# A hybrid layer on one core: in the recurrence, the two chunks of a block trade places for odd pairs of heads

## The chip, the cores and the metric

One core of a Trainium2 chip runs the whole layer. The metric is the device time of one execution in microseconds (us); before, it is 2475.47 us, the median of three runs. A profile of one execution stands beside it.

## What is computed

One decoder layer on 2048 tokens of 1024 channels: a mixer of two groups of heads (an SSD group and an RWKV-7 group), then a convolved GLU. The change lies in the RWKV-7 group. Cut to what matters here, its 8 heads of 64 channels each run this recurrence over the tokens:

```
def step(S, inp):                       # S: 64 x 64 for each head
    r_t, w_t, k_t, v_t, a_t, b_t = inp
    sa = jnp.einsum("bhij,bhj->bhi", S, a_t)
    S = S * w_t[:, :, None, :] + sa[..., None] * b_t[:, :, None, :] + v_t[..., None] * k_t[:, :, None, :]
    return S, jnp.einsum("bhij,bhj->bhi", S, r_t)
...
y = _rwkv7_scan(rh, heads(decay), kh, vh, -kk, kk * ah)
y = ((y - mean) * lax.rsqrt(var + RWKV_GN_EPS)).reshape(b, T, RWKV_D) * f32(ln_w) + f32(ln_b)
```

The vectors r, k, v, w, a and the gate come from projections of the normalised input (`xn @ w_in`) and small products behind them.

## The kernel before

The 2048 tokens are 16 **blocks** of 128; a block is two **chunks** of 64 tokens. The 8 heads are 4 **pairs** j, and hh (0 or 1) is the head within a pair. Tensors with channels on the 128 partitions (`tk`, `tr`, `tv`, `AR`, `BK`) hold a pair's two heads in the two halves of the partitions and the block's 128 tokens along the row, chunk 0 first.

Within a chunk the recurrence is solved in matrix form. `gram` makes the masked products `G` of a chunk (128 partitions: one half for the solved vectors U, one for the values V). `sides(c)` says which: for chunk 0 the U half is partitions 64 to 127 (`us`) and the V half 0 to 63 (`vs`), for chunk 1 the other way round. `UV[:, c]` holds U and V of a chunk in the same halves. Per chunk these steps follow each other; their products are small and in fp32, and the trace shows each fp32 product as two records:

- `own`: `local` (L1306) multiplies the V half of `G` by V, for the `us` and the `vs` columns of every head (16 products of 64 x 64 on a 64-column operand), into the bank `pq`; `past` (L1312) adds the state's part, 4 full products; then ScalarE copies the `us` half of `pq` to `qs` (L1318).
- `update`: 8 products with the inverse `XT` (L1330), all in the same 64 x 64 quarter of the array, into `pu`; ScalarE copies them to the U half of `UV` (L1334, one instruction of 64 x 512).
- `state`: `kept` on GpSimd scales the old state, `fresh` (L1354, `pS`, 8 products of 128 rows by 64 columns, left and right half of the array in turn), `join` on VectorE adds both (L1360); `reads` (L1365) multiplies the U half of `G` by U into the `vs` half of `pq`, 8 products in one and the same quarter; ScalarE copies that half to `ysb` (L1371).

`XT` comes from a chain of 62 small VectorE instructions for each block (`solve`, L1186 and L1192, `tmp` and `xl`), with DMAs before and behind; `turn` (L1257, `XW`, on VectorE) and `merge` (L1273 `pw`, L1277 `po`, tiles of 32 x 32 at opposite corners of the array: rows from 64 to columns from 96 and rows from 0 to columns from 32, and their mirror images) finish the inverse. `values` makes the centred V (L1239, `vt`, 4 full products) and the bonus (L1247, `bo`, one product on 512 columns). The big products are the projections `d` (to `tk`, `tr`, `tv` and others) and `c` (for the convolution), L735, 24 at a time.

TensorE's order is written out by hand. For blocks 1 to 13 a list (`PLAN`) interleaves, in one **period**, the steps of block f (`f.`), of the one behind it (`b.`) and of the one behind that (`a.`); the other engines issue in the order of the same list. So every engine runs its queue in order, and an instruction that waits holds back what stands behind it on its engine. In a period TensorE runs, in this order: `nq` (a norm), `local` of chunk 0, `c`, `past`, `c`, `pw`, `c`, `po`, `gr` (the gram), `pu`, `c`, `zg`, `pS`, `reads`, `c`, `local` of chunk 1, `past`, `bt`, `d`, `pu`, `bt`, `d`, `reads`, `pS`, `d`, `bo`, `d`, `yt`, `vt` and `d` to the next `nq`. Lists of their own (`HEAD`, `ORDER`) do the same for the start and the end. Behind the recurrence come the SSD chunks and the GLU.

Of the kernel before, what the change touches and what calls it, by code (L numbers as in the profile page):

```python
# [10 lines left out]
AF = mybir.ActivationFunctionType  # L11
# [7 lines left out]
P = 128  # L19
# [256 lines left out]
R0.merge.1/0 R1.gram.1/0 R1.conv.5/0 R0.merge.1/1 R0.update.0/0 R1.conv.5/1 R1.gram.1/1 R1.gram.1/2 R1.conv.3/8  # L276
R1.receptance/2 R2.load/0 R1.conv.3/9 R1.conv.6/0 R1.conv.3/10 R1.conv.1/11 R2.load/3 R1.receptance/4 R1.conv.5/2
R1.solve/0 R1.conv.5/4 R0.update.0/1 R1.conv.5/3 R1.conv.5/5 R1.receptance/3 R1.solve/1 R1.conv.5/7 R1.solve/3
R1.solve/2 R2.load/4 R1.conv.7/0 R1.conv.3/11 R1.solve/8 R2.load/5 R2.load/6 R0.state.0/2 R0.merge.1/2
R1.transposed.0/0 R1.conv.7/1 R1.conv.5/6 R1.conv.5/8 R0.state.0/5 R0.own.1/0 R1.d.10/0 R1.solve/4 R0.state.0/3  # L280
R1.conv.7/2 R1.conv.7/4 R0.state.0/4 R1.conv.7/6 R1.receptance/1 R0.state.0/6 R1.conv.7/3 R1.solve/7 R0.own.1/1
R2.load/7 R0.gate/0 R1.solve/5 R0.own.1/2 R0.update.1/0 R0.update.1/1 R0.state.1/5 R0.state.1/6 R0.finish.0/0
R0.state.1/0 R0.state.1/1 R1.solve/6 R1.d.11/0 R1.conv.7/8 R1.conv.7/5 R1.conv.7/7 R1.d.11/1 R1.solve/9 R1.solve/10
R1.solve/11 R1.conv.5/9 R1.solve/12 R1.solve/13 R1.solve/14 R1.solve/15 R1.solve/16 R1.solve/17 R1.solve/18
R1.solve/19 R1.solve/20 R1.solve/21 R1.solve/22 R1.solve/23 R1.solve/24 R1.solve/25 R1.solve/26 R1.solve/27
R1.solve/28 R1.solve/29 R1.solve/30 R1.solve/31 R1.conv.7/9 R0.state.1/2 R1.solve/32 R1.solve/33 R1.solve/34
# [33 lines left out]
f.d.11/1 f.solve/7 n.load/8 b.update.1/0 b.update.1/1 f.solve/9 f.d.11/2 f.solve/10 f.solve/11 f.solve/12 f.solve/13  # L320
f.solve/14 f.solve/15 f.solve/16 f.solve/17 f.solve/18 f.solve/19 f.solve/20 f.solve/21 f.solve/22 f.d.11/3 f.solve/23
f.solve/24 f.solve/25 f.solve/26 f.solve/27 f.solve/28 f.solve/29 f.solve/30 f.solve/31 f.solve/32 f.solve/33
f.solve/34 n.load/9 f.transposed.1/0 f.d.12 f.d.11/4 b.state.1/5 b.state.1/2 f.d.13/0
# [416 lines left out]
def phase_R(tc, K, const, tables, x, w_r, w_c, wl_d, g2_d, XN, XC, YR, iters=16):  # L740
    nc = tc.nc
    V, S, G_ = nc.vector, nc.scalar, nc.gpsimd
    with ExitStack() as ctx:
# [102 lines left out]
        def bank(name, tag, bufs=1):  # L846
# [1971 lines left out]
```

## Time and profile before

| | before |
|---|---|
| runs | 2476.57, 2471.09, 2475.47 us; median 2475.47 us |
| the profiled execution | 2477.94 us, its span 2476.2 us |
| TensorE busy | 2386.1 us, 96% of the span |
| VectorE, ScalarE, GpSimd busy | 1876.3, 1193.2, 1061.6 us |
| blocks 1 to 13 in their periods | from 149.3 to 802.4 us, about 50.3 us each |
| the recurrence with start and end | to about 900 us; then SSD chunks to about 1240 us, GLU to the end |

Engines are named PE (TensorE), PEld (its weight loads), DVE (VectorE), ACT (ScalarE), POOL (GpSimd). A row of a timeline gives a group's start, its time from first start to last end, engine, line, operation, output and inputs, shapes and the number of records; idle time before it and what ended it stand in brackets. Matmuls overlap: the time from one row's start to the next row's start is what a group costs TensorE.

### The profile page before, as it was taken

The page shows a single profiled execution, that of the slowest core. Times are in us where ns is not written, and L with a number is a line of the kernel's source. Part 1 is how long each engine was busy: PE and PEld are TensorE (multiplying, and loading weights), DVE is VectorE, ACT ScalarE, POOL GpSimd, SP SyncE. Part 2 cuts the span into 40 slices and gives each one's busy share as a digit, 9 for nine tenths or more (in the row PEclk, how much of TensorE's full clock was granted, in tenths as well). Part 3 has the DMA queues.
Part 4 walks back from the last instruction along what each step waited for, and adds up shares of the span by engine and source line. Part 5 has one row for each costly group of instructions (what it writes and reads, how often), then busy time and mean ns, then how long its engine had stood idle before and what let it go on. Part 6 is the DMA issues. An engine that isn't in the chain of part 4 may idle for free.

```text
span 2476.2 us, 53715 instructions
## 1 busy us (share of the span) xinstructions
PE 2386.1 (96%) x21212; PEld 1513.2 (61%) x21212; DVE 1876.3 (76%) x3790; ACT 1193.2 (48%) x2407; POOL 1061.6 (43%) x1134
## 2 busy tenths in 40 slices
PE   4999999999999999999988999999989999999998
PEld 4899999999999755555533444444434444444443
DVE  6878777878787667678999799988988645546457
ACT  7556665666666444445555544444543432313132
POOL 3334443444434522223335658576755432313225
PEclk8999999999999999999999999999999999999999
DMA  7432333223422546565775444534455453333243
GB/s 226 91 68 57 79 72 77 58 63 78 87 58 62 172 122 169 154 175 164 194 225 172 166 151 152 182 136 153 149 175 174 166 162 98 107 102 102 85 158 111
DMA packets 344412, 319.12 MB, mean 129 GB/s; under 512 B 203232, under 2 KB 248672, under 8 KB 340832
## 3 DMA queue, kind: packets, MB, share of 16 engines
q1 hardware_dynamic: 344016, 315.43, 43.6%
q8 instruction: 166, 2.72, 0.5%
q14 instruction: 86, 0.70, 0.1%
q10 hardware_dynamic: 144, 0.26, 0.0%
HBM read 187.85 MB, written 110.99 MB: 121 GB/s over the span
## 4 chain that ended last, share of the span: by engine, by line
PE 40%; DVE 7%; issue 3%; POOL 2%; DMA 2%; ACT 2%; SPq 0%; DVEq 0%; POOLq 0%; ACTq 0%
PE u L2250 25%; PE d L2490 12%; DVE w L2103 1%; PE o L1964 1%; DVE C L2272 1%; PE l L2615 1%; DVE p L2307 1%; DVE a L2307 1%; POOL fa L2101 1%; DMA hs<-HN 0%; PE z L1749 0%; DVE dw L2454 0%; DMA HN<-hT 0%; POOL m L2002 0%; ACT hl L1983 0%
## 5 line engine op out<-in xcount | busy, mean ns | idle before, releaser
L2250 PE MATMUL u<-b,w 128*128 128x512 f16 x3696 | 807.0, 380 | 17.7 <-DVE C L2272 7.6
L2250 PEld LDWEIGHTS <-w 128*128 128x128 f16 x3696 | 362.3, 98 | 457.2 <-issue 24.4
L735 PE MATMUL d<-xt,wr 128*128 128x129 f16 x5376 | 334.6, 224 | 27.4 <-DMA xt<-xh 14.1
L735 PEld LDWEIGHTS <-wr 128*128 128x128 f16 x5376 | 319.9, 100 | 41.2 <-issue 33.1
L2490 PE MATMUL d<-dw,fa 128*128 128x512 f16 x1512 | 334.6, 380 | 4.3 <-DVE dw L2454 3.5
L2490 PEld LDWEIGHTS <-fa 128*128 128x128 f16 x1596 | 156.4, 98 | 199.6 <-issue 12.5
L2272 DVE TENSOR_TENSOR C<-u,C 128x512 f32<-128x512 f32 x220 | 150.8, 686 | 158.9 <-PE u L2250 141.9
L735 PE MATMUL c<-xt,wc 128*128 128x131 f16 x3072 | 194.3, 224 | 5.9 <-ACT tv L965 2.9
L735 PEld LDWEIGHTS <-wc 128*128 128x128 f16 x3072 | 182.1, 98 | 10.7 <-issue 6.1
L2503 DVE TENSOR_TENSOR acc<-d,acc 128x512 f32<-128x512 f32 x212 | 139.7, 683 | 43.8 <-PE d L2490 39.6
L2101 POOL TENSOR_TENSOR fa<-p,fa 128x512 f16<-128x512 f32 x100 | 133.6, 1346 | 74.4 <-ACT fa L2096 74.4
L2307 DVE SCALAR_TENSOR_TENSOR p<-C,fpar,p 128x1024 f32<-128x1024 f32 x88 | 121.2, 1377 | 45.4 <-ACT p L2303 45.2
L2103 DVE SCALAR_TENSOR_TENSOR w<-us,w 128x512 f16<-128x512 f32 x132 | 127.6, 977 | 9.3 <-ACT w L2096 8.6
L1014 DVE SCALAR_TENSOR_TENSOR ca<-c,cw,ca 128x128 f32<-128x128 f32 x360 | 114.5, 345 | 25.7 <-ACT ca L1004 21.8
L2268 ACT ACTIVATE C<-u 128x512 f32<-128x512 f32 x88 | 52.2, 594 | 169.5 <-PE u L2250 127.2
L2307 DVE SCALAR_TENSOR_TENSOR a<-C,fpar,a 128x1024 f32<-128x1024 f32 x88 | 121.8, 1384 | 6.9 <-ACT a L2303 5.5
L1186 DVE TENSOR_TENSOR tmp<-atl,xl 128x60 f32<-128x60 f32 (+24 forms) x465 | 117.0, 252 | 11.5
L1192 DVE TENSOR_TENSOR xl<-xl,tmp 128x60 f32<-128x60 f32 (+24 forms) x465 | 111.2, 239 | 13.9
L2096 ACT ACTIVATE fa<-p 128x512 f16<-128x512 f32 x110 | 65.6, 622 | 114.9 <-DVE p L2320 87.7
L2096 ACT ACTIVATE w<-us 128x512 f16<-128x512 f32 x132 | 79.9, 623 | 81.5 <-PE u L2250 31.4
L2223 POOL TENSOR_TENSOR us<-us,us 128x512 f32<-128x512 f32 x51 | 78.1, 1533 | 50.0 <-DVE w L2103 29.5
L1749 PE MATMUL z<-ws,xs 128*128 128x512 f16 x384 | 92.5, 383 | 0.0
(334 smaller groups left out, 4229.6 us busy)
## 6 DMA issues: line engine op xcount, KB each, us to landing
UW<-w SPq DMA_DIRECT2D x154, 256.0 KB
w<-UW SPq DMA_DIRECT2D x154, 256.0 KB
us<-in_w_u_dram SPq DMA_DIRECT2D x88, 256.0 KB
DW<-dw SPq DMA_DIRECT2D x70, 256.0 KB
dw<-DW SPq DMA_DIRECT2D x56, 256.0 KB
hs<-HN SPq DMA_DIRECT2D x48, 256.0 KB
r<-in_w_d_dram SPq DMA_DIRECT2D x10, 1024.0 KB
xin<-in_x_dram SPq DMA_DIRECT2D x16, 512.0 KB
```

The costliest lines, as they stand in the source:

```text
L735: nc.tensor.matmul(ps, w[:, a, kt, :], xt[:, b, kt, cols], start=n == 0, stop=n == 3 * KT - 1)
L1014: V.scalar_tensor_tensor(out=acc[:, q], in0=m["rc", e][:, q, k:k + 128], scalar=cw[:, e + q, k:k + 1], in1=acc[:, q], op0=ALU.mult, op1=AL ...
L1186: chain.tensor_tensor(out=self.tmp[:, :k, :n], in0=self.atl[:, j, j + 1:32].unsqueeze(1).to_broadcast([P, k, n]), in1=self.xl[:, :k, j:j + ...
L1192: chain.tensor_tensor(out=self.xl[:, :k, j + 1:32], in0=self.xl[:, :k, j + 1:32], in1=self.tmp[:, :k, :n], op=ALU.add)
L2096: S.activation(h, src, AF.Copy, **({} if scale is None else {"scale": scale}))
L2101: {"V": V, "G": G_}[engine].tensor_tensor(out=l, in0=src, in1=h, op=ALU.subtract)
L2103: V.scalar_tensor_tensor(out=l, in0=src, scalar=scale, in1=h, op0=ALU.mult, op1=ALU.subtract)
L2250: nc.tensor.matmul(bk[at], self.w[i][:, u, k, :], self.half.b[i][:, k, v, :], start=start and n == 0, stop=n == 11, skip_group_check=True)
L2272: op("V", .61, lambda: V.tensor_tensor(out=part(j, x), in0=bk[at], in1=part(*a), op=ALU.add), (("u", 4 * s + at), (*(c0, c1)[a[0]], a[1])) ...
L2307: V.scalar_tensor_tensor(out=o[j], in0=C[j][:, 2 - d:1026 - d], scalar=cw(g, 2 - d), in1=o[j], op0=ALU.mult, op1=ALU.add)
L2490: nc.tensor.matmul(bk[s, t], pairs[m].a[i][:, u, t * P:t * P + P], pairs[m].w[n][0][:, v, :], start=new and m == 0 and u == v == 0, stop=m ...
L2503: V.tensor_tensor(out=acc[j][:, t], in0=bk[s, t], in1=acc[j][:, t], op=ALU.add)
```

## The change

For odd pairs j the two chunks of a block are stored in swapped places: chunk 1's tokens first. A step for chunk c then works at place `c ^ j % 2`, so even pairs use one half of the partitions for U and odd pairs the other. With the heads taken in the order 0, 2, 1, 3, 4, 6, 5, 7, products that follow each other in `local` and `update` lie in opposite quarters of the array.

- `d`, `low` (tanh) and `finish` (affine) read the odd pairs with the two halves of 64 tokens swapped (a view with a reversed step of 64), or write them back so: the same instructions with another view.
- `local` makes the `us` columns alone, 8 products for 16. `reads` takes all 128 rows of `G` (U and V part at once), 8 products of 128 rows by 64 columns, left and right half of the array in turn.
- `qs` copies all 128 partitions (128 x 512). The copies to `UV` and to `ysb` become two each (`put(0)`, `put(1)`, 64 x 256).
- `vt` becomes 8 products with 64 columns of weights; `bo` becomes 6 products, of 128, 64 and 64 columns and the same again. `kept` on GpSimd has a view with one more dimension.
- In the lists the second copies stand behind the first; `R0.merge.1/2`, `R14.values/2`, `R15.values/2` and `R15.merge.1/2` move forward.

```
+        ORDER8 = (0, 2, 1, 3, 4, 6, 5, 7)
+        def swap(t):
+            return t.rearrange("p (c t) -> p c t", t=64)[:, ::-1]
...
                 def own(u):
-                    S.activation(dst(u), m["d", e][:, u, 1:129], AF.Identity, scale=omu[:, e + u:e + u + 1])
+                    S.activation(put(u), got(m["d", e][:, u, 1:129], u), AF.Identity, scale=omu[:, e + u:e + u + 1])
...
                     for j in range(4):
-                        nc.tensor.matmul(ps[:, j, :], self.tv[:, j], cmat, start=True, stop=True)
+                        for i in range(2):
+                            o = 64 * (i ^ j % 2)
+                            nc.tensor.matmul(
+                                ps[64 * i:64 * i + 64, j, :], self.tv[:, j, o:o + 64], cmat, start=True, stop=True)
...
-                    nc.tensor.matmul(m["bo"], K.bones, self.tr, start=True, stop=True)
+                    for j in range(4):
+                        for a, b in (((0, P),), ((0, 64), (64, P)))[j % 2]:
+                            o = 64 - a if j % 2 else a
+                            nc.tensor.matmul(
+                                m["bo"][:, j, a:b], K.bones, self.tr[:, j, o:o + b - a], start=True, stop=True)
...
+            def heads(self, c):
+                for n, h in enumerate(ORDER8):
+                    j, hh = h // 2, h % 2
+                    yield n, h, j, hh, c ^ j % 2, slice(h * 64, h * 64 + 64)
...
-                        for o in (us, vs):
-                            nc.tensor.matmul(
-                                pq[o, h * 64:(h + 1) * 64], self.G[vs, c, hh, j, o], self.UV[vs, c, h * 64:(h + 1) * 64],
-                                start=h == 0, stop=False, skip_group_check=True)
+                    for k, h, j, hh, i, q in self.heads(c):
+                        us, vs = self.sides(i)
+                        nc.tensor.matmul(
+                            pq[us, q], self.G[vs, i, hh, j, us], self.UV[vs, i, q], start=k < 2, stop=False,
+                            skip_group_check=True)
...
-                    S.activation(m["qs", c][us], m["pq", c][us], AF.Copy)
+                    S.activation(m["qs", c], m["pq", c], AF.Copy)
...
-                            pu[us, h * 64:(h + 1) * 64], self.XT[us, 4 * hh + j, :], m["qs", c][us, h * 64:(h + 1) * 64],
-                            start=True, stop=True)
-                return [products, lambda: S.activation(self.UV[us, c, :], m["pu", c][us], AF.Copy)]
+                            pu[us, q], self.XT[us, 4 * hh + j, :], m["qs", c][us, q], start=True, stop=True)
+                def put(b):
+                    us, vs = self.sides(c ^ b)
+                    S.activation(pick(self.UV[us, c ^ b, :], b), pick(m["pu", c][us], b), AF.Copy)
+                return [products, lambda: put(0), lambda: put(1)]
...
-                            m["pq", c][vs, h * 64:(h + 1) * 64], self.G[us, c, hh, j, vs],
-                            self.UV[us, c, h * 64:(h + 1) * 64], start=False, stop=h == 7, skip_group_check=True)
+                            m["pq", c][vs, q], self.G[:, i, hh, j, vs], self.UV[:, i, q], start=False, stop=k > 5,
+                            skip_group_check=True)
```

TensorE in the middle of a period, where `pS` and `reads` of chunk 0 stand between the gate `zg` and a group of `c`. Before:

```order
L735 MATMUL c_4_7938<-xt_6477,wc 128x131
L1380 MATMUL zg_8069<-GL_6402,g_200 128x128 x4
L1354 MATMUL pS_8078<-UV_7646,BT_7423 64x64 x8
L1365 MATMUL pq_7758<-UV_7646,G_7002 64x64 x8
L735 LDWEIGHTS wc
```

Now:

```order
L737 MATMUL c_4_7921<-xt_6471,wc 128x131
L1414 MATMUL zg_8053<-GL_6392,g_200 128x128 x4
L1386 MATMUL pS_8062<-UV_7637,BT_7405 64x64 x8
L1396 MATMUL pq_7749<-UV_7637,G_6989 64x64 x8
L737 LDWEIGHTS wc
```

Nothing moves there; `reads` (L1396, before L1365) keeps its number of products and has the shape of `pS` now. Then TensorE at chunk 1's `local` and `past`. Before:

```order
L735 MATMUL c_6_8110<-xt_6477,wc 128x131
L1306 MATMUL pq_8166<-UV_7646,G_7002 64x64 x16
L1312 MATMUL pq_8166<-S_1_228,AR_6953 128x128 x4
L1226 MATMUL bt_7_8194<-cst,BK_7886 128x128 x4
L735 LDWEIGHTS wr
```

Now:

```order
L737 MATMUL c_6_8094<-xt_6471,wc 128x131
L1334 MATMUL pq_8151<-UV_7637,G_6989 64x64 x8
L1340 MATMUL pq_8151<-S_1_228,AR_6939 128x128 x4
L1243 MATMUL bt_7_8171<-cst,BK_7869 128x128 x4
L737 LDWEIGHTS wr
```

The 16 products are 8 at the same place. Last, ScalarE between the copy to `UV` and the copy to `ysb` of chunk 0; `xh` and `xin` load the next block's input. Before:

```order
L1334 ACTIVATE UV_6616<-pu_6980 64x512
L916 ACTIVATE xh_6998,ss_6999<-xin_6956 128x1024
L1020 ACTIVATE ct_2_7045<-ca_2_6950 128x256
L1004 ACTIVATE ca_4_7066<-c_4_6908,cb,cw 128x128
L935 ACTIVATE xin_6956<-xin_6956,pnr_7013 128x1024
L936 ACTIVATE xh_6998<-xin_6956 128x1024
L1004 ACTIVATE ca_4_7066<-c_4_6908,cb,cw 128x128
L1382 ACTIVATE tg_7107<-zg_7039 128x512
L1371 ACTIVATE ysb_7134<-pq_6728 64x512
L1004 ACTIVATE ca_6_7161<-c_6_7080,cb,cw 128x128 x2
```

Now:

```order
L1362 ACTIVATE UV_6610<-pu_6966 64x2x128 x2
L926 ACTIVATE xh_6985,ss_6986<-xin_6942 128x1024
L1036 ACTIVATE ct_2_7032<-ca_2_6936 128x256
L1020 ACTIVATE ca_4_7053<-c_4_6894,cb,cw 128x128
L945 ACTIVATE xin_6942<-xin_6942,pnr_7000 128x1024
L946 ACTIVATE xh_6985<-xin_6942 128x1024
L1020 ACTIVATE ca_4_7053<-c_4_6894,cb,cw 128x128
L1416 ACTIVATE tg_7094<-zg_7026 128x512
L1402 ACTIVATE ysb_7121<-pq_6722 64x2x128 x2
L1020 ACTIVATE ca_6_7141<-c_6_7067,cb,cw 128x128 x2
```

Each copy is two, in the place of the one. VectorE, GpSimd and the DMA queue keep their order throughout, and TensorE and ScalarE theirs from the SSD chunks on.

## Rows read from the trace of the kernel before

**Rows 1.** The page's 40 slices of the span (62 us each): busy tenths of TensorE, and the granted clock of TensorE in tenths.

```profile
PE   4999999999999999999988999999989999999998
...
PEclk8999999999999999999999999999999999999999
```

**Rows 2.** Busy time by stretch: stretch, its length, then busy us (and instructions) of PE, PEld, DVE, ACT, POOL, then granted clock, DMA share and GB/s. The stretch before block 1, two periods, and the two stretches behind the periods.

```profile
110.00:149.40 39.40, 37.95 (x595) 35.18 (x596) 28.87 (x107) 21.51 (x51) 13.67 (x14) 1.00 0.33 66
149.40:199.70 50.30, 50.30 (x852) 47.38 (x854) 39.78 (x129) 31.17 (x71) 21.32 (x24) 1.00 0.30 64
...
400.70:451.00 50.30, 50.30 (x850) 47.36 (x849) 39.84 (x130) 31.16 (x71) 21.28 (x24) 1.00 0.32 71
...
803.10:853.40 50.30, 47.15 (x696) 39.91 (x694) 31.87 (x85) 25.64 (x52) 30.43 (x73) 1.00 0.57 183
853.40:900.00 46.60, 42.13 (x383) 26.25 (x382) 29.40 (x69) 24.77 (x62) 12.09 (x13) 0.92 0.48 147
```

**Rows 3.** TensorE's timeline in one period (the sixth), from `local` of chunk 0 to the product behind `vt`.

```profile
400.71 1.15 PE L1306 MATMUL pq<-UV,G 64*64 64x64 f32 x32
...
408.44 0.83 PE L1273 MATMUL pw<-XW,G 32*32 32x32 f32 x32
...
410.71 0.69 PE L1277 MATMUL po<-XT,XW 32*32 32x32 f32 x32
411.33 2.08 PE L1146 MATMUL gr<-AR,BK 64*128 64x128 f32 x32
413.35 1.14 PE L1330 MATMUL pu<-qs,XT 64*64 64x64 f32 x16
414.42 1.57 PE L735 MATMUL c<-xt,wc 128*128 128x131 f16 x24
...
416.87 0.69 PE L1354 MATMUL pS<-UV,BT 128*64 128x64 f32 x16
417.49 1.14 PE L1365 MATMUL pq<-UV,G 64*64 64x64 f32 x16
418.56 2.97 PE L735 MATMUL c<-xt,wc 128*128 128x131 f16 x48
421.46 1.15 PE L1306 MATMUL pq<-UV,G 64*64 64x64 f32 x32
422.54 1.16 PE L1312 MATMUL pq<-S,AR 128*128 128x128 f32 x8
...
431.56 4.31 PE L735 MATMUL d<-xt,wr 128*128 128x129 f16 x72
435.70 1.08 PE L1247 MATMUL bo<-tr,cst 128*128 128x512 f32 x2
436.68 1.54 PE L735 MATMUL d<-xt,wr 128*128 128x129 f16 x24
...
438.49 1.06 PE L1239 MATMUL vt<-cmat,tv 128*128 128x128 f32 x8
439.39 1.54 PE L735 MATMUL d<-xt,wr 128*128 128x129 f16 x24
```

**Rows 4.** TensorE's timeline in the SSD part: fp32 products with full weights on 64 columns.

```profile
878.73 1.90 PE L1881 MATMUL py<-Xdt,Dt 128*128 128x64 f32 x16
```

**Rows 5.** Operations with views in several pieces and plain ones beside them (groups by line with their shapes: busy us, mean ns of one).

```profile
L1123 POOL TENSOR_TENSOR BK<-tk,Pv 128x512 f32<-128x512 f32 x16 | 21.2, 1322 | 2.5 <-PE nq L1100 1.9 <-DVE tk L1116 0.6
L1428 POOL TENSOR_TENSOR yln<-yln,tv 128x512 f32<-128x512 f32 x16 | 20.8, 1302 | 69.4 <-ACT yln L1418 69.4
L1133 DVE TENSOR_TENSOR AR<-tr,Pi 128x512 f32<-128x512 f32 x16 | 10.8, 674 | 0.0
L1758 ACT ACTIVATE sz<-z 128x512 f32<-128x512 f32 x16 | 9.5, 593 | 12.4 <-PE z L1749 12.4
```

**Rows 6.** ScalarE's timeline in the same period, from the copies behind `pw` to the first instruction of the last group of `c`.

```profile
409.43 0.76 ACT L1284 ACTIVATE XW<-pw 32x256 f32<-32x256 f32 x2
...
414.53 0.59 ACT L1334 ACTIVATE UV<-pu 64x512 f32<-64x512 f32 x1 [2.32 <-PE pu L1330]
415.14 1.06 ACT L916 ACTIVATE xh<-xin 128x1024 bf16<-128x1024 f32 x1
...
420.48 0.58 ACT L1371 ACTIVATE ysb<-pq 64x512 f32<-64x512 f32 x1
421.57 0.81 ACT L1004 ACTIVATE ca<-c,cb,cw 128x128 f32<-128x128 f32 x2 [0.51 <-PE c L735]
```

**Rows 7.** VectorE's timeline in the same period: from the norm behind `nq` to `XW`, then from the first instruction behind the last `c` to the one that `nq` of the next period waits for by way of ScalarE.

```profile
404.87 0.69 DVE L1113 SCALAR_TENSOR_TENSOR kkn<-sq,kkn 128x512 f32<-128x512 f32 x1 [1.85 <-ACT sq L1112]
...
407.63 0.90 DVE L1257 STREAM_TRANSPOSE XW<-XT 32x256 f32<-32x256 f32 x2
...
422.41 2.15 DVE L1014 SCALAR_TENSOR_TENSOR ca<-c,cw,ca 128x128 f32<-128x128 f32 x6 [0.70 <-ACT ca L1004]
...
428.88 0.35 DVE L968 SCALAR_TENSOR_TENSOR tv<-d,mus,tv 128x128 f32<-128x128 f32 x1 [0.83 <-ACT tv L965]
...
432.14 0.34 DVE L968 SCALAR_TENSOR_TENSOR tv<-d,mus,tv 128x128 f32<-128x128 f32 x1
...
441.63 0.61 DVE L968 SCALAR_TENSOR_TENSOR tk<-d,mus,tk 128x128 f32<-128x128 f32 x2 [0.24 <-ACT tk L965]
...
448.62 0.34 DVE L968 SCALAR_TENSOR_TENSOR tr<-d,mus,tr 128x128 f32<-128x128 f32 x1
```

More of the change, by code (lines that the diff above doesn't have):

```diff
@@ L275 @@
 R1.norm/12 R0.merge.0/2 R1.conv.3/4 R0.merge.0/1 R1.gram.0/0 R1.gram.0/1 R1.conv.3/7 R1.gram.0/2 R2.load/2 R1.conv.3/6
[L276 to L279, printed above, removed]
+R0.merge.1/0 R1.gram.1/0 R1.conv.5/0 R0.merge.1/1 R0.merge.1/2 R0.update.0/0 R1.conv.5/1 R1.gram.1/1 R1.gram.1/2
@@ L282 @@
[L282 to L286, printed above, removed]
@@ L320 @@
[L320 to L323, printed above, removed]
+f.d.0 b.solve/35 a.state.1/6 a.state.1/7 b.solve/36 b.solve/37 a.finish.0/0 b.solve/38 f.d.1/0 b.d.13/2 b.conv.7/9
@@ L324 @@
+f.solve/25 f.solve/26 f.solve/27 f.solve/28 f.solve/29 f.solve/30 f.solve/31 f.solve/32 f.solve/33 f.solve/34 n.load/9
+f.transposed.1/0 f.d.12 f.d.11/4 b.state.1/5 b.state.1/2 f.d.13/0
 """
@@ L437 @@
-R15.solve/73 R15.solve/71 P1.steps/1 X.wo.2/0 R15.solve/74 R15.solve/72 R14.finish.1/3 R14.finish.1/4 R14.finish.1/5
-R14.finish.1/6 R15.conv.7/10 X.left/11 P0.flip/2 R15.own.0/2 C0.z.3/3 R15.solve/75 R15.solve/76 C2.z.1/0 C0.rows/0
-R15.conv.7/11 R15.turn/1 C2.z.2/0 C2.z.3/0 R15.turn/0 R15.merge.0/0 X.wo.2/1 R15.conv.5/11 C0.decay.0/0 R15.solve/77
-C1.z.3/2 R15.state.0/0 R15.merge.0/1 R15.merge.0/2 C0.begin/1 X.left/12 R15.solve/78 X.wo.3/0 R15.merge.1/0
-R15.state.0/1 C0.decay.0/1 R15.merge.1/1 C0.decay.0/2 C0.off/0 C2.z.3/1 C0.decay.0/3 C0.decay.0/4 R15.update.0/0
@@ new lines @@
+R15.solve/39 R15.solve/40 R15.solve/41 X.wo.0/0 P0.steps/1 R15.solve/42 R15.conv.3/8 P0.steps/2 R15.solve/43 X.wz.2/4
+X.wz.2/2 R15.solve/44 R15.solve/45 R15.solve/46 R15.solve/47 R14.finish.0/2 R14.finish.0/3 X.left/1 X.wz.3/3
+R15.solve/48 C0.begin/0 R15.conv.1/10 R15.conv.3/9 R15.solve/49 X.wz.3/2 R15.conv.3/10 P0.steps/3 R15.conv.6/0
+R15.conv.7/0 R15.conv.1/11 X.left/4 X.wz.3/4 C0.z.2/0 C0.z.3/0 X.left/5 R15.solve/50 R15.conv.5/1 R15.conv.5/2
+R15.conv.7/1 R15.conv.7/2 R15.own.0/0 R15.solve/51 R15.solve/52 R15.solve/53 R15.solve/54 R15.conv.5/3 R15.conv.7/3
@@ new lines @@
+P0.flip/1 X.wo.1/1 R15.solve/69 P1.steps/0 C1.z.3/1 P0.sums/2 R14.finish.1/1 R14.finish.1/2 R15.conv.7/9 X.wo.1/2
+X.left/9 R15.conv.5/10 C2.z.0/0 P1.load.1/0 R15.solve/70 R15.solve/73 R15.solve/71 P1.steps/1 X.wo.2/0 R15.solve/74
+R15.solve/72 R14.finish.1/3 R14.finish.1/4 R14.finish.1/5 R14.finish.1/6 R15.conv.7/10 X.left/11 P0.flip/2 R15.own.0/2
+C0.z.3/3 R15.solve/75 R15.solve/76 C2.z.1/0 C0.rows/0 R15.conv.7/11 R15.turn/1 C2.z.2/0 C2.z.3/0 R15.turn/0
+R15.merge.0/0 X.wo.2/1 R15.conv.5/11 C0.decay.0/0 R15.solve/77 C1.z.3/2 R15.state.0/0 R15.merge.0/1 R15.merge.0/2
@@ new lines @@
+C0.begin/1 X.left/12 R15.solve/78 X.wo.3/0 R15.merge.1/0 R15.state.0/1 C0.decay.0/1 R15.merge.1/1 R15.merge.1/2
+C0.decay.0/2 C0.off/0 C2.z.3/1 C0.decay.0/3 C0.decay.0/4 R15.update.0/0 C3.z.0/0 C0.begin/2 X.wo.3/1 X.wo.2/2
+C0.decay.0/6 C0.decay.0/7 R15.update.0/1 R15.update.0/2 X.wo.3/2 C0.off/1 C0.decay.1/0 C0.decay.1/1 R15.state.0/2
+X.wo.4/0 C0.decay.1/2 C0.decay.1/3 R15.state.0/3 X.wo.5/0 C0.decay.1/4 R15.state.0/5 R15.state.0/4 R14.finish.1/7
+C0.decay.0/5 C0.decay.1/5 C3.z.1/0 R15.own.1/0 R15.own.1/1 C0.decay.1/6 R15.state.0/6 R15.state.0/7 C0.decay.1/8
```

230 lines of the change are left out of this document (120 added, 110 removed).

## The prediction

> **What bounds the kernel now.** I read the page's slices first: from the second slice on, TensorE is busy in nine tenths or more of nearly every one, and its granted clock is at nine tenths or more, the level of 2.4 GHz [rows 1]. The busy times by stretch say it more sharply: in a period of blocks 1 to 13 TensorE is busy 50.30 of 50.30 us, VectorE 39.8, ScalarE 31.2, GpSimd 21.3, at a clock of 1.00; before the periods it has 1.5 us of idle time, behind them 3.15 of 50.3 and 4.47 of 46.6 us [rows 2]. So in 13 periods, from 149.3 to 802.4 us, each microsecond that TensorE saves shortens the kernel, until it has to wait for an engine that so far was always ahead. The SSD and GLU parts keep their code. The question is therefore, first, what the small products cost TensorE, and second, how far ahead of it the others are.
>
> The first is read from the starts in TensorE's timeline [rows 3]. Two groups of 16 records with 64 columns stand side by side: `pS`, 128 rows in alternating column halves, goes from 416.87 to 417.49, 0.62 us; `reads`, all in one quarter, from 417.49 to 418.56, 1.07. `pu`, also in one quarter, takes 1.07 (413.35 to 414.42). `local` has 32 records and takes 1.08 (421.46 to 422.54): it goes from one column half to the other after each product, and comes to the cost of paired records, 0.034 each. Products that use different parts of the array thus overlap, and those in the same part don't (0.067).
>
> **Does it hold for opposite quarters,** with other rows too, and writing other halves of one bank? The nearest row is `po`: 32 records of 32 x 32 in opposite corners, in one bank, 0.62 us (410.71 to 411.33) [rows 3], under 20 ns each. On half the columns of `pS`, that is half its price per record, so they overlap. I take 0.62 for 16 such records; the other end is 1.07.
>
> **TensorE's sum for one block.**
> - `local`: 16 products become 8, 32 records become 16. In overlap 1.08 becomes 0.62: -0.46, twice a block -0.92. The other end: 8 unpaired products cost what `pu` does, 1.07, no gain.
> - `update`: 1.07 becomes 0.62: -0.45, twice -0.90. The other end is 0.
> - `reads`: as many products, now of the shape of `pS`, and next to it, so that the change of shape between them goes too. `pS` has its own change in its 0.62; 16 records of 0.62/16 = 0.039 at most, less about 0.09 for a change: 0.53 in place of 1.07, -0.54, twice -1.08. (The 0.09 is worked out from `pu`: first to last end is 1.14, one record alone some 0.22, so 15 more at 0.061, and 16 times that is 0.98 of the 1.07.) It rests on the shape of its neighbour, and is the surest term. Without the change saved it is -0.45.
> - `bo`: one product on 512 columns (435.70 to 436.68, 0.98) becomes 6, 12 records. A full product in fp32 has a floor: `py`, 16 records with full weights on 64 columns, takes 1.90 first to last end [rows 4], less some 0.27 for one alone, 0.109 each; `vt`, on 128 columns, takes 0.90 for 8, 0.113 each [rows 3]. So 12 x 0.11 = 1.31: +0.33. The bounds are 0 (columns alone count) and +0.4.
> - `vt`: 8 records in 0.90 become 16 with half the weight columns. Paired they cost as before, 0.9, with 0.1 to 0.2 for the change of shape (`gr`, 32 records on 128 columns in row halves, 2.02, gives 1.01 for 16); unpaired 1.8. I take +0.2, from `gr` as the nearest; the bounds are 0 and +1.0.
>
> The sum is -0.92 - 0.90 - 1.08 + 0.33 + 0.2 = -2.4 us a block.
>
> **The other engines' edits.** ScalarE's copies to `UV` and `ysb` become two each, on half the columns. `XW`, two pieces, takes 0.76 where one copy of 64 x 512 takes 0.59 [rows 6]: +0.06 to +0.17 each; I take +0.12. ScalarE has 19 us free in a period, but two of these copies are waited for, below. `qs` on 128 rows for 64: `sz` at 128 x 512 takes 593 ns [rows 5] where the 64-row copies take 0.58 and 0.59 [rows 6]: nothing. GpSimd's `kept` has one dimension more: `BK`, whose views are split in pieces, takes 1322 where the plain `yln` takes 1302 ns; VectorE's `AR` from split views takes 674 [rows 5] where the plain `kkn` takes 0.69 us [rows 7]: nothing, and GpSimd has 29 us a period to hide it. The reversed views, in 6 `past` on VectorE and some 12 instructions on ScalarE per block, I cost at nothing as well, by the same rows; no row shows a step that goes backward, and the third rival prices that. No DMA is added, moved or passed. In the lists only steps of blocks 0, 14 and 15 move.
>
> **What is late next.** I followed how far each wait in a period is from becoming one.
> 1. Chunk 1's `local` writes the bank that `ysb` must have emptied. `ysb` ends at 420.48 + 0.58 = 421.06 [rows 6], `local` starts at 421.46 [rows 3]: 0.40 to spare. By then TensorE is 0.45 + 0.54 = 0.99 ahead (`pu`, `reads`). ScalarE gains `pu`'s 0.45 at the `UV` copy, loses some 0.12 to each second copy, and in between waits for GpSimd's `pnr` (0.43 idle before `xin`) [rows 6], which starts no earlier than ScalarE's own `xh`: I take 0.25 at the end of `ysb`. So 0.65 of the 0.99 gets through; 0.35 is lost.
> 2. Then `local`, `pu` and `reads` of chunk 1 add 0.46 + 0.45 + 0.54: 2.1 ahead within the `d` group of 431.56. Its 24 records behind the first 48 start at some 432.94, and their bank must have been read by `tv`, which ends at 432.14 + 0.34 = 432.48 [rows 7]: 0.46 to spare. VectorE, in order, comes there after ten microseconds of `ca` and `solve`: it starts them 0.65 earlier at 422.41, and can use up the 0.83 of idle time before the `tv` at 428.88, less what that one's product lags: some 1.4. So TensorE may be 1.9 ahead; 0.2 is lost.
> 3. `bo` and `vt` give back 0.5: about 1.35 ahead. VectorE can use 0.24 more before `tk` at 441.63, and its last `tr` at 448.62 [rows 7] leaves 2.0 us to the next `local`, at 450.99.
> 4. In the next period chunk 0's `local` would add 0.46. But `pw` stands behind `XW`, 407.63 + 0.90 = 408.53 on VectorE [rows 7], later than `pw`'s first record at 408.44: its second half waits already (0.83 for `po`'s 0.69, of the same shape) [rows 3]. `XW` stands behind `kkn`, which waits 1.85 for ScalarE [rows 7], and that for `nq`, ahead of `local` on TensorE. So `XW` comes earlier by what TensorE gained before `nq`, not by `local`: 0.46 is lost.
>
> What is left of a period: 2.4 - 0.35 - 0.2 - 0.46 = 1.35 to 1.4. I take 1.35; times 13 it is -17.5. Blocks 0, 14 and 15 save TensorE another 7, but it has 1.5, 3.15 and 4.47 us of waits there [rows 2], for other engines and for transfers: I take -1. In all -18.5. The profiled execution's 2477.94 becomes 2459.4; it lay 2.5 over the median of the runs, so I predict 2475.5 - 18.5 = **2457 us**.
>
> **The rivals.**
> *A, the waits don't appear.* If the transfers of time among the engines are kinder (ScalarE's `ysb` early enough, `XW` pulled along), the whole sum comes through: 13 x 2.4 + 2 = 33, **2442**. For it: each of the three margins is under half a microsecond, and a few hundred nanoseconds on ScalarE remove one. Against: `pw`'s second half waits already.
>
> *B, opposite quarters don't overlap.* If products from different rows into one bank run one after the other, `local` and `update` keep 1.07, and `reads` alone gains 1.08 against the 0.53 of `bo` and `vt`: 0.55 a block, of which the wait for `ysb` and ScalarE's longer copies leave some 0.2, times 13: 2.6, **2473**. The half-microsecond groups of `po` speak against it [rows 3]. The Trainium skill, "TensorEngine Tiling (Array Packing)", section "Gotcha 1: PSUM Pressure", states this as a rule: different row tiles cannot access the same PSUM bank at once. By that rule the change would come to this rival's time; `po`, with corners of different rows into one bank, doesn't bear it out.
>
> *C, slower: a view that steps backward is dear.* Six `past` a block run with one on VectorE, between the `solve` instructions on which `XW` and `tv` hang. Each takes 0.34 now [rows 7]. If such a view doubled it, 6 x 0.35 = 2.1 us would be added to VectorE's chain in a period, whose free idle time (0.83 and 0.24) the forecast has used up: 2.1 against 1.35 is +0.75, times 13 +10, **2485**. It decides from 1.35/6 = 0.23 us an instruction. For it: no row shows one. Against: views in pieces cost 0 to 2% [rows 5].
>
> **How the numbers follow.** About 0.2%, 5 us, is what a measurement of this kernel can tell from no change. The forecast has 0.63; A 0.17; B 0.07; C 0.06; and 0.07 goes to waits that take back more than I found (each 0.1 us a period is 1.3 us; half a microsecond gives 2463 to 2470). The range runs from a little beyond A to 2469, which takes in the 1.07 end of `update` or the dear end of `vt` (0.8 x 13 = 10, 2467): 2440 to 2469, leaving out B and C and the tails. Faster by over 0.2%: 0.63 + 0.17 + 0.05 = 0.85; within 0.2%: B and the end of the rest, 0.08; slower: C and a little, 0.07.
>
> **What the changed profile would show.** Right: a period of 48.9 us for 50.28; `local`, `pu` of 16 records in about 0.62, `reads` in 0.53 behind `pS`; `bo` near 1.3, `vt` near 1.1; TensorE idle before chunk 1's `local`, ended by `ysb`, within `d`, ended by `tv`, and longer before `pw`, ended by `XW`, 0.2 to 0.5 each, with TensorE at some 97 to 98% of a period. A shows as a period of 47.9 without these waits; B as groups of 1.07 for `local` and `pu`; C as `past` instructions in two lengths on VectorE. I'd be wrong in kind if ScalarE's second copies, or a wait in the chain from `nq` to `XW`, cost TensorE more than 1.4 us in a period.

## The result, and the profile after

The changed kernel takes 2460.52 us, the median of four runs (2457.07 to 2461.38), where the kernel before takes 2476.02 (2471.09 to 2477.12). The ratio is 0.9939, with a 95% interval of 0.9921 to 0.9956: 0.6% faster. Timed again (the eighth experiment) it was 2462.03 against 2478.01, a ratio of 0.9935 (0.9916 to 0.9955).

TensorE's timeline in the sixth period of the changed kernel, from `nq` to the next; it answers to [rows 3]. A period is now 443.91 - 394.56 = 49.35 us.

```profile
394.56 1.13 PE L1117 MATMUL nq<-sq,cst 128*128 128x512 f32 x2
395.62 0.68 PE L1334 MATMUL pq<-UV,G 64*64 64x64 f32 x16
396.23 2.97 PE L737 MATMUL c<-xt,wc 128*128 128x131 f16 x48
...
403.03 0.24 PE L1297 MATMUL pw<-XW,G 32*32 32x32 f32 x2
403.49 0.69 PE L1297 MATMUL pw<-XW,G 32*32 32x32 f32 x30 [0.22 <-DVE XW L1281]
404.11 1.57 PE L737 MATMUL c<-xt,wc 128*128 128x131 f16 x24
...
408.25 0.68 PE L1357 MATMUL pu<-qs,XT 64*64 64x64 f32 x16
408.87 1.57 PE L737 MATMUL c<-xt,wc 128*128 128x131 f16 x24
...
411.31 0.69 PE L1386 MATMUL pS<-UV,BT 128*64 128x64 f32 x16
411.83 0.64 PE L1396 MATMUL pq<-UV,G 128*64 128x64 f32 x16
412.40 2.97 PE L737 MATMUL c<-xt,wc 128*128 128x131 f16 x48
415.78 0.68 PE L1334 MATMUL pq<-UV,G 64*64 64x64 f32 x16 [0.41 <-ACT ysb L1402]
...
424.34 1.55 PE L737 MATMUL d<-xt,wr 128*128 128x129 f16 x24
426.27 2.94 PE L737 MATMUL d<-xt,wr 128*128 128x129 f16 x48 [0.38 <-DVE tv L984]
429.04 1.50 PE L1270 MATMUL bo<-tr,cst 128*128 128x128 f32 x12
430.40 1.54 PE L737 MATMUL d<-xt,wr 128*128 128x129 f16 x24
431.78 0.60 PE L1449 MATMUL yt<-cst,ysb 128*128 128x128 f32 x4
432.32 1.09 PE L1258 MATMUL vt<-cmat,tv 128*64 128x128 f32 x16
433.34 1.55 PE L737 MATMUL d<-xt,wr 128*128 128x129 f16 x24
...
443.91 1.12 PE L1117 MATMUL nq<-sq,cst 128*128 128x512 f32 x2
444.96 0.68 PE L1334 MATMUL pq<-UV,G 64*64 64x64 f32 x16
```

Read from start to start: `local` takes 0.61, `pu` 0.62, `pS` and `reads` together 1.09 (1.69 before), `bo` 1.36, `vt` 1.02. Three groups carry idle time in brackets that no group had before. Busy time by stretch for one such period, with the columns of [rows 2], has TensorE at 48.22 of 49.30 us, 98%, where it was at 100:

```profile
395.60:444.90 49.30, 48.22 (x835) 45.41 (x834) 39.83 (x130) 31.54 (x75) 21.23 (x23) 1.00 0.32 72
```

The waits of TensorE over the 13 periods (who waits, for what, total us, times, the longest). One more, a single wait of 0.2 us, is left out. The list has idle times of over 0.15 us; in the kernel before it is empty:

```profile
PE pq L1334 <- ACT ysb L1402: 5.4, 13, 0.4
PE d L737 <- DVE tv L984: 4.9, 13, 0.4
PE pw L1297 <- DVE XW L1281: 2.6, 12, 0.2
```

How much each takes back shows against the kernel before, by distance from chunk 0's `local` (400.71 before, 395.62 after). Rows of before that stand in no group above, the `c` behind chunk 0's `local`, the `c` behind `pw`, `nq` and the next period's `local`:

```profile
401.79 2.97 PE L735 MATMUL c<-xt,wc 128*128 128x131 f16 x48
...
409.21 1.57 PE L735 MATMUL c<-xt,wc 128*128 128x131 f16 x24
...
449.94 1.12 PE L1100 MATMUL nq<-sq,cst 128*128 128x512 f32 x2
451.00 1.15 PE L1306 MATMUL pq<-UV,G 64*64 64x64 f32 x32
```

| place | before | after | ahead by |
|---|---|---|---|
| `c` behind chunk 0's `local` | 1.08 | 0.61 | 0.47 |
| `c` behind `pw` | 8.50 | 8.49 | 0.01 |
| `c` behind `reads` of chunk 0 | 17.85 | 16.78 | 1.07 |
| `local` of chunk 1 | 20.75 | 20.16 | 0.59 |
| `d` behind `pS` of chunk 1 | 30.85 | 28.72 | 2.13 |
| `bo` | 34.99 | 33.42 | 1.57 |
| `d` behind `vt` | 38.68 | 37.72 | 0.96 |
| the next `local` | 50.29 | 49.34 | 0.95 |

So the wait for `XW` costs 0.46, the one for `ysb` 0.48, the one within `d` 0.56, and `bo` and `vt` 0.6.

The queues behind two of these waits, ScalarE's and then VectorE's timeline of the changed kernel. `tg` is ScalarE's copy of `zg`; `xh` belongs to the next block's input:

```profile
408.98 0.77 ACT L1362 ACTIVATE UV<-pu 64x256 f32<-64x256 f32 x2 [1.87 <-PE pu L1357]
409.65 1.04 ACT L926 ACTIVATE xh<-xin 128x1024 bf16<-128x1024 f32 x1
...
414.49 0.59 ACT L1416 ACTIVATE tg<-zg 128x512 f32<-128x512 f32 x1
414.97 0.76 ACT L1402 ACTIVATE ysb<-pq 64x256 f32<-64x256 f32 x2
...
421.41 0.78 ACT L1362 ACTIVATE UV<-pu 64x256 f32<-64x256 f32 x2 [0.25 <-PE pu L1357]
422.21 0.37 ACT L981 ACTIVATE tv<-d,omu 128x128 f32<-128x128 f32 x1
```
```profile
422.61 0.35 DVE L984 SCALAR_TENSOR_TENSOR tv<-d,mus,tv 128x128 f32<-128x128 f32 x1 [0.38 <-ACT tv L981]
...
425.87 0.34 DVE L984 SCALAR_TENSOR_TENSOR tv<-d,mus,tv 128x128 f32<-128x128 f32 x1
```

`local` starts as soon as the second `ysb` copy ends (414.97 + 0.76 = 415.73). The second `tv` on ScalarE starts 0.80 after the first of the two copies to `UV` of chunk 1; in the kernel before, the same pair of rows on ScalarE stands 0.50 apart:

```profile
428.00 0.59 ACT L1334 ACTIVATE UV<-pu 64x512 f32<-64x512 f32 x1 [0.70 <-PE pu L1330]
428.50 0.35 ACT L965 ACTIVATE tv<-d,omu 128x128 f32<-128x128 f32 x1
```

At chunk 0's copies to `UV` the difference is smaller: `xh` starts 0.67 behind the first of the two, 0.61 behind the one of before [rows 6]. The 0.83 of VectorE's idle time at the first of the `tv` above [rows 7] is 0.38, and still ended by ScalarE.

**Behind the periods.** The last `nq` of the recurrence starts at 800.49 before and at 788.42 after: the periods, with the start, are worth 12.1 us of the 16.6 by which the spans differ. From there to the end it is 1675.7 before and 1671.2 after. This stretch has the same instructions as before in the seventh experiment, where it takes 1670.7, and the same as after in the third to sixth, the eighth and the ninth, where it takes 1676.3, 1672.1, 1670.1, 1672.7, 1670.1 and 1674.5. The 4.5 us lie within what it varies by; no gain or loss there is shown.

### The profile page after: what moved, and what is told of

Same layout as the page of the kernel before. It is cut to its first block, busy times and chain, and to the rows that moved or that the text cites. A ratio compares the mean times of both kernels' runs of the same rounds, so it can differ in the third digit from the quotient of the medians.

```text
span 2459.6 us, 53351 instructions
## 1 busy us (share of the span) xinstructions
PE 2353.0 (96%) x20986; PEld 1483.9 (60%) x20988; DVE 1879.6 (76%) x3790; ACT 1200.3 (49%) x2471; POOL 1061.2 (43%) x1134
## 4 chain that ended last, share of the span: by engine, by line
PE 40%; DVE 7%; issue 3%; POOL 3%; ACT 2%; DMA 2%; SPq 0%; POOLq 0%; DVEq 0%; ACTq 0%
PE u L2288 25%; PE d L2528 12%; DVE w L2141 1%; PE o L2002 1%; PE l L2653 1%; DVE C L2310 1%; DVE p L2345 1%; DVE a L2345 1%; POOL fa L2139 0%; DMA hs<-HN 0%; PE z L1787 0%; POOL m L2040 0%; DVE dw L2492 0%; DMA HN<-hT 0%; DVE b L2139 0%
## 5 line engine op out<-in xcount | busy, mean ns | idle before, releaser
L1203 DVE TENSOR_TENSOR tmp<-atl,xl 128x60 f32<-128x60 f32 (+24 forms) x465 | 129.0, 277 | 11.7 <-DMA atl<-ATd 0.2
L1209 DVE TENSOR_TENSOR xl<-xl,tmp 128x60 f32<-128x60 f32 (+24 forms) x465 | 99.2, 213 | 13.9
```

The lines of the kernel that those rows point to most:

```text
L1203: chain.tensor_tensor(out=self.tmp[:, :k, :n], in0=self.atl[:, j, j + 1:32].unsqueeze(1).to_broadcast([P, k, n]), in1=self.xl[:, :k, j:j + ...
L1209: chain.tensor_tensor(out=self.xl[:, :k, j + 1:32], in0=self.xl[:, :k, j + 1:32], in1=self.tmp[:, :k, :n], op=ALU.add)
```

## The experiments

A period's length is that of most of the 13, from `nq` to `nq`. These agree within 0.03 us; the first and the last are up to 1.4 us shorter, now and then one more strays (in the fourth one has 49.94 and one 49.30; why is open), and the ninth has two lengths. Runs 1 to 5 are one execution each, too few to tell 6 us by the whole time, so their periods are compared; the whole times are 2470.43, 2460.01, 2459.78, 2455.86 and 2451.53 us. Runs 1 to 4 shared a chip, so did 5 to 8. Code is cut with "...", and cuts out of the list of a period break their lines elsewhere than the list.

**1. The same quarter.** `local` and `update` take four heads of one quarter, then four of the other.

```diff
+        SAME8 = (0, 1, 4, 5, 2, 3, 6, 7)
...
-                    for k, h, j, hh, i, q in self.heads(c):
+                    for k, h, j, hh, i, q in self.heads(c, SAME8):
...
-                            pq[us, q], self.G[vs, i, hh, j, us], self.UV[vs, i, q], start=k < 2, stop=False,
+                            pq[us, q], self.G[vs, i, hh, j, us], self.UV[vs, i, q], start=k % 4 == 0, stop=False,
```

> The theory on the products: what makes local and update cheaper is that successive products lie in opposite quarters, each on its own rows and its own half of one bank. The rival: it is the halved count of local, and something in the new layout for update, and the order of the heads does not matter. Here local and update take four heads of one quarter and then four of the other; all else, reads too, stays. Theory: a group of 16 records goes from 0.62 back to 1.0 to 1.07 us (one overlap at the seam). Chunk 0's local hides in the wait for XW (0.37 now), so a period goes from 49.35 to 50.3 to 50.7 us, 0.42 for each of the other three groups less what the waits before local and within d give. Rival: groups of 0.62, a period of 49.35.

Measured: a period of 50.18 us. TensorE's timeline, chunk 0's `local` and `update`:

```profile
398.05 0.96 PE L1335 MATMUL pq<-UV,G 64*64 64x64 f32 x16
398.94 2.97 PE L737 MATMUL c<-xt,wc 128*128 128x131 f16 x48
...
410.69 0.96 PE L1358 MATMUL pu<-qs,XT 64*64 64x64 f32 x16
411.58 1.57 PE L737 MATMUL c<-xt,wc 128*128 128x131 f16 x24
```

A group takes 0.89, 0.27 more than in the changed kernel, and three such groups make nearly all of the 0.83 by which the period is longer; the fourth, chunk 0's `local`, hides in the wait for `XW`. The order of the heads alone makes the overlap, so the theory on the products holds; the seam of the two quarters gives more back (0.18) than I expected. The single records show how: in the kernel before, those of `pu` start 58 ns apart; in the changed one two start within 7 ns, and the pairs 58 ns apart; here the first record of the second quarter starts beside the fifth of the first, ahead of the three behind that one.

**2. `bo` and `vt` in whole products,** so that the values of odd pairs stand in the wrong places.

```diff
-                        for i in range(2):
-                            o = 64 * (i ^ j % 2)
...
+                        nc.tensor.matmul(ps[:, j, :], self.tv[:, j], cmat, start=True, stop=True)
...
+                    nc.tensor.matmul(m["bo"], K.bones, self.tr, start=True, stop=True)
```

> bo is one product on 512 columns again and vt four full ones; the values of the odd pairs then stand in the wrong places, which leaves the amount of work elsewhere as it is. bo goes from 1.36 to 0.98 us, vt from 1.02 to 0.90 with 0.1 less ahead of it. Theory on the waits: these two stand behind the wait within d and ahead of nq, and what hangs on nq comes earlier with it, so the whole 0.6 comes through: a period of 48.75 us for 49.35. Rival, VectorE's own chain sets the period by now: it has 0.48 of idle time before tk and none behind it, so at most 0.5 comes through, and if the chain from the wait within d to nq is full, 0.0 to 0.2: 49.15 to 49.35.

Measured: 49.10 us, between the two. The timeline behind the wait within `d`:

```profile
424.58 1.08 PE L1264 MATMUL bo<-tr,cst 128*128 128x512 f32 x2
425.94 1.54 PE L737 MATMUL d<-xt,wr 128*128 128x129 f16 x24 [0.28 <-DVE tv L984]
```

`vt`'s share came through; `bo`'s did not: the next `d` waits for the two `tv` behind it on VectorE. So the dearer `bo` cost the change almost nothing: it filled a wait. My theory had missed that one.

**3, 4 and 5. The three waits, one at a time.** Each moves steps in the list of a period; the products stay. In the third ScalarE makes its second `tv` (`f.d.11/2`) ahead of the copies to `UV`, in the fourth its copies to `ysb` (`b.state.0/6` and `/7`) ahead of `tg` (`b.gate/1`), and in the fifth VectorE turns `XW` (`b.turn`) earlier:

```diff
-f.d.11/1 f.solve/7 n.load/8 b.update.1/0 b.update.1/1 b.update.1/2 f.solve/9 f.d.11/2
+f.d.11/1 f.d.11/2 f.solve/7 n.load/8 b.update.1/0 b.update.1/1 b.update.1/2 f.solve/9
...
-b.gate/1 f.conv.7/0 b.state.0/3 b.state.0/6 b.state.0/7
+f.conv.7/0 b.state.0/3 b.state.0/6 b.state.0/7 b.gate/1
...
-b.solve/76 f.conv.1/5 f.conv.1/7 b.conv.7/11 f.conv.2 b.turn/0 b.solve/78 b.turn/1
+b.solve/76 b.turn/0 b.turn/1 f.conv.1/5 f.conv.1/7 b.conv.7/11 f.conv.2 b.solve/78
```

> In a period, ScalarE makes the second of its two tv instructions of d group 11 ahead of the two copies to UV of chunk 1, not behind them. Theory on the waits: TensorE's wait within d (idle 0.38, 0.55 lost against the kernel before) stands there because the second copy holds up tv by 0.3 us, and with it VectorE's queue; VectorE is idle for 0.38 at that place and can come 0.38 earlier. The wait then goes to nearly 0, and a period from 49.35 to 49.0 us. Rival, VectorE's queue is bound by what stands ahead of it: the wait stays and the period is 49.35.

> In a period, ScalarE makes its two copies to ysb of chunk 0 ahead of tg (128x512, 0.48 us from start to start), not behind it. Theory on the waits: local of chunk 1 waits 0.41 for ysb; that wait goes to 0, TensorE is 0.41 earlier, and VectorE has 0.38 of idle time behind it to follow, so the wait within d stays what it is or grows by little: a period of 48.95 to 49.0 us for 49.35. Rival, the loop through VectorE sets the period: the wait within d grows by 0.4 and the period stays at 49.35.

> In a period, VectorE turns XW two instructions (0.5 us) earlier, ahead of the last two of the five ca that stood before it; its other instructions follow in their order. Theory on the waits: pw loses 0.15 and 0.22 us to XW; both go, and what TensorE gains in chunk 0's local comes through for the first time: a period of 48.95 to 49.0 us for 49.35. Rival, VectorE's queue is full and takes it back within d: the wait for tv there grows from 0.38 to 0.75 and the period stays at 49.35.

Measured: 48.87, 48.89 and 48.80 us, so 0.48, 0.46 and 0.55 less a period. In none of the three did the period stay at 49.35, so each rival falls. In the third the 72 records of `d` run in one group; in the fourth `local` follows `c` without a wait, and the wait within `d` is as it was; in the fifth `pw` has none, a new one of 0.24 for `ca` stands behind it, and the wait for `ysb` has shrunk. TensorE's timelines, one fence each:

```profile
421.52 4.37 PE L737 MATMUL d<-xt,wr 128*128 128x129 f16 x72
```
```profile
412.62 0.68 PE L1334 MATMUL pq<-UV,G 64*64 64x64 f32 x16
...
423.13 2.93 PE L737 MATMUL d<-xt,wr 128*128 128x129 f16 x48 [0.40 <-DVE tv L984]
```
```profile
398.03 0.69 PE L1297 MATMUL pw<-XW,G 32*32 32x32 f32 x32
398.97 1.56 PE L737 MATMUL c<-xt,wc 128*128 128x131 f16 x24 [0.24 <-DVE ca L1030]
...
410.37 0.68 PE L1334 MATMUL pq<-UV,G 64*64 64x64 f32 x16 [0.16 <-ACT ysb L1402]
```

The last brings 0.2 more than I expected: 0.3 at `pw`, and 0.25 at `ysb`, where GpSimd's `pnr` (a 128 x 1 instruction for the next block's input), which ScalarE's `xin` waits for, took 0.57 for 0.82 us. Why it was shorter there I did not test.

**6. All three.**

> The three moves of order at once: tv ahead of the copies to UV, ysb ahead of tg, XW earlier. The theory on the waits has to reckon with VectorE: tv first and ysb first each used up the same 0.38 us of its idle time ahead of tv (0 is left there in both), so together they bring little more than one of them, 0.48 to 0.55, and the move of XW adds its 0.37, since all that follows it hangs on TensorE: a period of 48.4 to 48.5 us, some 11 to 12 us less than the changed kernel as it is. Rival, the waits are independent: 49.35 - 0.48 - 0.46 - 0.37 = 48.04, 17 us less.

Measured: 2449.43 us, a ratio of 0.9888 (0.9868 to 0.9908) to the kernel before, where the changed kernel beside it has 0.9935; a period of 48.35, 0.05 under what the theory has, and not 48.04. VectorE's idle times from the last `ca` on, and TensorE at `d`:

```profile
458.21 2.16 DVE L1030 SCALAR_TENSOR_TENSOR ca<-c,cw,ca 128x128 f32<-128x128 f32 x6 [0.40 <-ACT ca L1020]
476.76 0.61 DVE L984 SCALAR_TENSOR_TENSOR tk<-d,mus,tk 128x128 f32<-128x128 f32 x2 [0.48 <-ACT tk L981]
```
```profile
467.43 2.92 PE L737 MATMUL d<-xt,wr 128*128 128x129 f16 x48 [0.16 <-DVE tv L984]
```

Between them VectorE has no idle time of over 0.15 us left, and TensorE waits for it: 0.15 to 0.16 of idle time in most periods, by which the record of `d` there starts 0.31 later than records of `d` otherwise follow each other. (The idle time of 0.32 that the ninth's expectation has stands in the one period of 48.51.) The wait for `ca` behind `pw`, new in the fifth, stays as well: 2.9 us over 12 of the 13 periods, here and in the ninth. No run takes it out.

**7. The same three moves in the kernel before** (its `b.gate/1` behind `b.state.0/6`).

> The same three moves of order in the kernel before. Theory on the waits: there TensorE waits in a period for none of them but 0.14 us in pw, so the moves are worth 0.14 or less: a period of 50.1 to 50.3 us, the time of the whole within 0.2%. Rival, the moves are better orders in themselves: 49.4 or less, 0.4% to 0.5% faster.

Measured: 2475.28 us, a ratio of 0.9990 (0.9980 to 1.0001), a period of 50.04, 0.24 less where I allowed 0.14: `pw` runs in 0.63, and `bo` and `nq` each in some 0.05 less. The moves are worth 0.24 us a period there and 1.0 in the changed kernel. Some three quarters of what they bring is thus not a better order in itself; it took the faster products to make the waits.

**8. The changed kernel again.**

> The changed kernel as it is, beside the others on one chip. Both theories: a period of 49.35 us, the whole 0.5% to 0.6% under the kernel before. It shows also how far the stretch behind the periods, whose code is the same in all of these, moves from one execution to the next: 1671 to 1677 us behind the last nq so far.

Measured: 2462.03 us and a period of 49.37; behind the last `nq` 1670.1 us.

**9. `tv` earlier on VectorE too,** on top of the three moves.

```diff
-f.solve/33 f.solve/34 n.load/9 f.transposed.1/0 f.d.12 f.d.11/4
+f.d.11/4 f.solve/33 f.solve/34 n.load/9 f.transposed.1/0 f.d.12
...
-b.solve/45 b.solve/46 a.finish.0/2 b.transposed.0/2 b.d.13/3 b.values/3 b.d.13/4
+b.d.13/3 b.d.13/4 b.solve/45 b.solve/46 a.finish.0/2 b.transposed.0/2 b.values/3
```

> The three moves, and on VectorE the second tv of d group 11 one pair of solve instructions (0.48 us) earlier, the two tv of group 13 likewise; VectorE does the same work in a period. Theory, VectorE's queue is full ahead of tv and TensorE waits 0.32 there because of what stands before tv, not because VectorE's whole loop is too long: the wait goes, a period of 48.03 for 48.35 us, another 4 us of the whole, some 0.988 - 0.002 = 0.987 of the kernel before. Rival, VectorE's loop as a whole sets the period: the wait comes back at XW or tk, and the period stays at 48.35.

Measured: 2448.66 us, a ratio of 0.9886 (0.9863 to 0.9909), no different from the sixth. The wait within `d` is gone, but most periods are 48.45 us and some 48.06, on average 48.28 as in the sixth. The last group of `d` and the `nq` behind it, and VectorE's next idle times after the `ca`:

```profile
415.55 4.32 PE L737 MATMUL d<-xt,wr 128*128 128x129 f16 x72
...
430.48 4.30 PE L737 MATMUL d<-xt,wr 128*128 128x129 f16 x72
434.89 1.13 PE L1117 MATMUL nq<-sq,cst 128*128 128x512 f32 x2
```
```profile
408.29 2.15 DVE L1030 SCALAR_TENSOR_TENSOR ca<-c,cw,ca 128x128 f32<-128x128 f32 x6 [0.40 <-ACT ca L1020]
434.36 0.35 DVE L984 SCALAR_TENSOR_TENSOR tr<-d,mus,tr 128x128 f32<-128x128 f32 x1 [0.43 <-ACT tr L981]
```

From 408.3 to 433.9 VectorE never waits, and what TensorE gained in the middle it loses ahead of `nq` (4.41 from start to start where the same group took 4.14). The loss stands at `nq` itself: it starts 0.33 behind the last record of `d`, 0.06 otherwise, and is released by ScalarE's `sq`, which follows the `tr` above. So the wait came back, though at `nq` and not at `XW` or `tk`, where the rival has it. In most periods the rival holds: over half a period VectorE's queue is now what sets the time.

## Why the prediction came out as it did

**The sum for TensorE was right.** -0.47 for each `local`, -0.45 for each `update`, -0.60 for each `pS` with `reads`, +0.38 for `bo`, +0.22 for `vt` with the `yt` ahead of it: -2.44, where the prediction had -2.4 (`reads` gained 0.06 more than its term, `bo` cost 0.05 more). Opposite quarters overlap as the rows of `po` said, so rival B is out. The rule of the Trainium skill that stands beside it ("TensorEngine Tiling (Array Packing)", "Gotcha 1: PSUM Pressure", that different row tiles can't access one PSUM bank at once) does not agree with this trace: records on different rows, into the two partition halves of one bank, start within 7 ns of each other, and 16 take 0.62 us where 16 in one quarter take 1.07.

**The three waits came where the prediction put them,** and rival A, which had none of them, is out. The one for `XW` took all of chunk 0's `local`, 0.46 as predicted. The one for `ysb` took 0.48 for 0.35: the end of `ysb` came 0.24 earlier (0.25 predicted, by other parts: the second copy to `UV` cost 0.06 and the one to `ysb` 0.18, for 0.12 each), and the rest is that `local` now starts 0.05 behind that end and `reads` had gained more.

**The step that failed is the second of "What is late next": VectorE "some 1.4" ahead at `tv`, 0.2 lost.** It was 1.2 ahead, and 0.56 was lost. I had let VectorE use up its 0.83 of idle time, but that time ended with ScalarE's `tv`, and ScalarE's `tv` stands behind the copies to `UV`. I priced the second copy by busy time, +0.12; this `tv` it held back by what it adds from start to start, 0.30. The rows close on it: the copies start 1.50 ahead of the kernel before (25.79 us behind chunk 0's `local`, 27.29 before), the `tv` behind them 1.20. Why the same second copy costs `xh` only 0.06 is not shown. The third experiment shows the place: `tv` ahead of the copies gives 0.48 back, more than the 0.36 that I was off. So the gain of a period was 0.93 and not 1.35, and 13 of them with the start gave 12.1 us and not 17.5.

**One margin of the list was misread, without harm.** The prediction gives VectorE's last `tr` 2.0 us to the next `local`. But ScalarE's `sq`, behind that `tr`, releases `nq`, which stands ahead of `local`; in the kernel before it ends at 449.89, 0.05 ahead of `nq`:

```profile
449.27 0.62 ACT L1091 ACTIVATE sq<-kkn 128x512 f32<-128x512 f32 x1
```

The same 0.05 stands in nearly every period of both kernels. It cost the changed kernel at most 0.02 us a period: VectorE's way to `sq` starts at `tk`, where it still waits for a `d` of TensorE and so comes as much earlier as that. The ninth experiment ran into it.

**The median came nearer than its parts.** 2457 was forecast, 2460.5 measured: the periods fell short by 5.4 us. For blocks 0, 14 and 15 I had 1 us; the pair of profiles shows 4.5 behind the periods, but that stretch varies by 6 us among kernels that have the same code there, so that part is neither confirmed nor refuted.

**Rival C is out:** the `tv` and `tr` on VectorE take 345 and 347 ns on average in both kernels, the reversed views among them, and ScalarE's 361 and 366 before, 364 and 366 after. The rest of what was costed at nothing held too: `qs` on 128 rows 595 ns for 592, `tS` on GpSimd 647 for 641.

## What to carry to other kernels

When an engine that is busy all the time gets faster, its gain is cut by the margins of the engines that release its buffers, so list those margins in order of time and subtract as you go; here three waits, none with more than half a microsecond to spare before, took 1.5 of 2.4 us a period. Price an added instruction on the releasing engine by how much later the one behind it starts, not by its busy time; the same pair of copies cost 0.06 at one place and 0.30 at another. Then move the releases forward in the order: three such moves were worth 0.24 us a period in the kernel before and 1.0 in the changed one, which they brought from 0.9935 to 0.9888.

## What the runs showed of the hardware

- TensorE starts small fp32 products of opposite quarters in pairs, within 7 ns, 58 ns from pair to pair, as it does single ones of one quarter, though they write the two halves of the same bank.
- It reaches ahead over three records for this: with four heads of one quarter in a row, the first record of the other quarter started beside the fifth of the eight, ahead of the sixth to eighth.
- The second of two ScalarE copies of 64 x 256, in place of one of 64 x 512, held back the next instruction by 0.30 us before `tv`, by 0.18 before `y` (behind chunk 1's `ysb`) and by 0.06 before `xh`; the halves take 377 ns each on average, the whole 591.
